# A hybrid decoder layer: a third tile for raw weights in the paired projections, two scratch rows claimed at once by each GLA pair, head 0's value parts issued behind the last sums of x, and two requeued steps in the DeltaNet part

## The chip, the cores and the metric

The kernel runs on one core of a Trainium2 chip. The metric is device time in microseconds of one execution, the median of several runs. PE is the matrix engine, DVE the vector engine, ACT the scalar engine, POOL the GpSimd engine and SP the engine that here only issues DMAs.

## The reference

One layer of a decoder: 512 tokens with 16 meta tokens ahead, width 2048. The normalised input goes through one combined projection, whose columns feed three kinds of heads; the gated results go through one output projection, a residual and a last norm.

```python
h = rms_norm(x, norm_w); h = pad(h)
proj = h @ w_in
(dq, dk, dv, dz, db, da, gq, gk, gv, gz, gl, fq, fk, fv, fz, ff) = split_cols(proj)
# A) 6 heads: gated DeltaNet (conv + SiLU on q, k, v; triangular solve in each chunk of 64)
o_dn = gated_head_norm(gated_delta_rule_chunked(q_dn, k_dn, v_dn, log_a, beta), dz, dn_norm_w)
# B) 5 heads: GLA, decay per key dimension
log_g = log_sigmoid(gl @ w_gk2 + b_gk) / 16
o_gla = gated_head_norm(gla_chunked(gq * 64**-0.5, gk, gv, log_g), gz, gla_norm_w)
# C) 5 heads: softmax attention with forget-gate bias, in blocks of 128 queries
o_fox = forgetting_attention(fq * 128**-0.5, fk, fv, log_f) * silu(fz)
return rms_norm(x + concat([o_dn, o_gla, o_fox]) @ w_out, final_norm_w)
```

All of it is float32. The chunk form of A needs the inverse of a lower triangular matrix per head and chunk.

## The kernel before

**Projections.** Each block of 128 projection columns is a product with K = 2048. A float32 operand is split into two parts, a rounded one and the rest (hi, lo), and three products of parts are summed: hi x hi, hi x lo of x, lo of the weights x hi. Weights come in halves of 128 x 1024: `load_half` (line 142) has SP load `raw`, ACT copy it into `whi` (line 162) and DVE subtract that into `wlo` (line 163). These two are put ahead of other work of their engines by a priority. The pool of these tiles, `wp`, holds two buffers of each name. `inproj` gives 96 matmuls for a block (line 220); a half-length matmul moves 264 columns, one without the meta tokens 512. `evac` brings the sum from PSUM to SBUF on DVE (line 338), `gate_z` does so for a gate (line 365) and applies SiLU through POOL and ACT (lines 347 to 351).

**Pairs of projections.** For heads 1 to 4 of the attention the blocks are computed two at a time by a scheme with seven products in place of eight (`inproj_pair`, line 505). `product` (line 513) is one of them: one `load_half`, then 24 matmuls (line 518). The scheme needs sums of halves of the weights, which POOL has added up in DRAM by DMA earlier (`ti`), and sums of halves of x: `x_sums` (line 472) prepares three sums per k and is called from the GLA pairs and head 0; `x_last` (line 493) then turns the second halves of x itself into differences, in place in `xh` and `xl`. Each k of `x_last` is a load on POOL (line 497), ACT 499, DVE 500, ACT 502, DVE 503. After it no ordinary projection may read that part of x, so it comes behind the last of them.

**The order of the work.** Two groups (g = 0, 1) of three DeltaNet heads come first. In each: gates, `dn_keys` (line 583), values, queries, `dn_inverse` (line 654), `dn_mix`. Then the gates of the GLA heads, three GLA pairs (`gla_pair`, line 860; the third pair has one head), and the attention heads (`fox_head`, line 1041). Independent chains run beside the projections on the other engines. Each engine works through a queue in order. A scheduler builds the queues from the written order and priorities; some matmuls are set behind a given projection matmul by hand (`behind`, `place`). A tile belongs to a buffer of its pool, and whoever first writes a new tile waits for the last users of the tile before it in that buffer. Of the tag `row` (128 x 531, scratch for one head's row) there are 7 buffers, of `six` (three rows) 14, of `t15` 6. PSUM has four banks for projections (`psb`) and four for all else (`psm`).

**DeltaNet keys.** `dn_keys` projects three key blocks with convolution and SiLU, then reads the decays `gb` from DRAM, broadcast over partitions (line 591, on ACT's queue), and forms the decay matrices on DVE from it: `atm` for the meta block and `at` for the four others (line 615), with ACT's exponentials (line 616).

**The inverse.** `dn_inverse` inverts the 32 x 32 diagonal blocks by elimination on DVE, writes them to DRAM and reads them back in two layouts, `xc` (a quarter of the tile `iv`) and `xm` (lines 682 and 684). DVE transposes both (lines 686, 687: `um`, `uc`), and matmuls `pm`, `pl`, `pn`, `pu` join the blocks.

**A GLA pair.** `gla_pair` projects keys and queries into the tile `gqk`, calls `x_sums`, projects two value blocks and turns them by PE (`pvg`, `pwg`, lines 853 and 856) into `gvt`. The gate's logarithms are computed in a row `u` with help of a row `t` (lines 883 to 892: `pgk` on PE, DVE, ACT, DVE). Then the scores come in seven steps (line 917 on): each has differences on DVE (922, 924), an exponential on ACT (925), products on DVE (926, 930) and small matmuls `pss` (944). The differences `d` stand in turn in the third part of `gvt` and in `u`. A third row, `spare`, is claimed ahead of the diagonal term (`psd`). After the scores: state updates (`pkd`, `pgm`, `pg`, `pgn`), the outputs `pgo` (lines 1008, 1014), the norm on ACT (1020 to 1025), and a transpose `pgt` (1028). SP reads the stored gate over the values in `gvt` (line 1031), DVE multiplies (1032) and SP stores the result in `zd` (1035).

**Attention head 0.** It uses ordinary projections: `fk`, `fv` into the row `vf`, `fq`, the gate `fz`, and head 1's `fk` and `fq` ahead. `values(v)` (line 1046) turns v by PE (`pvf`), splits it (`vhi`, `vlo`, `v3`, two rows and a small tile) and brings the meta values by `pwf`. The attention runs in four query blocks: logits `pfa` and `pfd` on PE (1118, 1119), the softmax on DVE and ACT (1122 to 1132), the transposes `pfx` (1135), the split of the probabilities (1138, 1139). After the blocks come `pfw` and the product `pfo`.

Of the kernel before, what the change touches and what calls it, by code (L numbers as in the profile page):

```python
# [8 lines left out]
F32 = mybir.dt.float32  # L9
# [9 lines left out]
P = 128  # L19
# [3 lines left out]
S = 512  # L23
T = NM + S
# [3 lines left out]
H = 3  # L28
# [54 lines left out]
def tile_hybrid_trunk(ctx, tc, xT, xtok, mtok, w_gate, w_in, w_out, w_dn, consts, lmask, fin_w, out, dbg=None):  # L83
# [57 lines left out]

    def load_half(src, name):
        raw = wp.tile([P, 1024], F32, tag="raw", name=f"raw{name}")
        nc.sync.dma_start(out=raw, in_=src)
        hi = wp.tile([P, 1024], F32R, tag="hi", name=f"whi{name}")
        lo = wp.tile([P, 1024], F32R, tag="lo", name=f"wlo{name}")
        split(raw, hi, lo)
        due[0] += rate[0]
        while due[0] > 0 and chores:
            cost = next(chores[0], None)  # L150
            if cost is None:
                chores.pop(0)
            else:
                due[0] -= cost
        return hi, lo
# [4 lines left out]
    def split(raw, hi, lo):  # L160
        with tc.high_priority(offset=1000000):
            pace[0] = A.copy(hi, raw).ins  # L162
            pace[1] = V.tensor_tensor(out=lo, in0=raw, in1=hi.bitcast(F32), op=ALU.subtract).ins  # L163

    pace = [None, None]

# [326 lines left out]
    def x_last():  # L493

        for k in range(NK):
# [7 lines left out]
            V.tensor_tensor(out=xl[k][:, HT:], in0=x22, in1=xh[k][:, HT:].bitcast(F32), op=ALU.subtract)  # L503

    def inproj_pair(n, c1, c2, tmp):

# [6 lines left out]
        def product(p_, src, xx, first=False, cols=slice(0, HT)):  # L513

            hi, lo = load_half(src, f"{b1}_{len(order)}")
            todo = [(hi, j, i) for j in range(NK) for i in range(2)] + [(lo, j, 0) for j in range(NK)]
            for i, (wt, j, part_) in enumerate(todo):
                m = PE.matmul(p_[:, cols], wt[:, j * P : (j + 1) * P], xx[j][part_][:, cols],  # L518
                              start=first and i == 0, stop=i == len(todo) - 1, skip_group_check=True)
                order.append(m.ins)  # L520
# [62 lines left out]
    def dn_keys(g):  # L583

        st = {}
        hs = range(H * g, H * g + H)
        kT = six.tile([P, H, T], F32, tag="six", name=f"kT{g}")
        for j, h in enumerate(hs):
            conv_silu(("dk", h), 6 + h, kT[:, j])
        gb = six.tile([P, H, T], F32, tag="six", name=f"gb{g}")  # L590
        nc.scalar.dma_start(out=gb, in_=gd[6 + H * g : 6 + H * g + H, :].partition_broadcast(P))
        kd = six.tile([P, NN, P], F32, tag="six", name=f"kd{g}")
# [61 lines left out]
    def dn_inverse(g, st):  # L654
# [30 lines left out]
        um = t15(f"um{g}", (32, H, 32))  # L685
        V.transpose(um.rearrange("p h c -> p (h c)"), xm.rearrange("p h c -> p (h c)"))
        V.transpose(uc.rearrange("p n c -> p (n c)"), xc.rearrange("p n c -> p (n c)"))

# [172 lines left out]
    def gla_pair(p):  # L861
# [12 lines left out]
        vt = vt3[:, :2, :S]  # L874
        V.memset(vt3[:, 0, 0:1], 0.0)
        x_sums(XSUM.get(p, ()))
        vm = t15(f"gvm{p}", (NM, 2, P))
        for e in range(ne):
            tok_values(inproj(("gv", 2 * p + e)), f"g{2 * p + e}", (vt3, qk)[e][:, 2], vt[:, e], vm[:, e])

        u = row(f"gu{p}")[:, :T][:R]
        t = row(f"gt{p}")[:, :T][:R]
        for a in range(2):
# [19 lines left out]

        spare = row(f"gpr{p}")[:, :S]
        prod = spare[:R]
# [7 lines left out]
        def scores(s, li):  # L913
            npair = S // (2 * s)
            kx, qx = kts[li % 2][:R], qts[li % 2][:R]
            v4 = lambda t_: t_.rearrange("p (n h s) -> p n h s", h=2, s=s)
            gv, kv, qv = v4(gc[:, NM:]), v4(kT[:, NM:]), v4(qT[:, NM:])
            kxv, qxv = v4(kx), v4(qx)
            d = (vt3[:R, 2, :S], u[:, :S])[li % 2]
            dv = v4(d)  # L920
            ref = gv[:, :, 0, s - 1 : s].to_broadcast([R, npair, s])
            V.tensor_tensor(out=dv[:, :, 1, :], in0=gv[:, :, 1, :], in1=ref, op=ALU.subtract)
            if s > 1:
                V.tensor_tensor(out=dv[:, :, 0, :], in0=ref, in1=gv[:, :, 0, :], op=ALU.subtract)
                A.activation(d, d, AF.Exp, scale=SC)
                V.tensor_tensor(out=kxv[:, :, 0, :], in0=kv[:, :, 0, :], in1=dv[:, :, 0, :], op=ALU.mult)
            else:
                A.activation(dv[:, :, 1, :], dv[:, :, 1, :], AF.Exp, scale=SC)
                kx = kT[:, NM:]
            V.tensor_tensor(out=qxv[:, :, 1, :], in0=qv[:, :, 1, :], in1=dv[:, :, 1, :], op=ALU.mult)  # L930
            return kx, qx
# [108 lines left out]
    def fox_head(h):  # L1040
# [24 lines left out]
        if h < H1:  # L1065
# [3 lines left out]
            x_sums(XSUM.get(3, ()))  # L1069
            vhi, vlo, v3, vm = values(v)  # L1070
            evac(inproj(("fq", h), meta=False), qT, scale=float(P) ** -0.5)
# [23 lines left out]
        if h < H1:  # L1095
            gate_z("fz", h, z)
            evac(inproj(("fk", H1)), ahead_[H1][:, 0])
            evac(inproj(("fq", H1), meta=False), ahead_[H1][:, 2], scale=float(P) ** -0.5)
            x_last()
        else:  # L1100
            zs["fz", h] = z
# [59 lines left out]
    XSUM = {1: (0, 1, 2), 2: (3, 4, 5), 3: (6, 7)}  # L1161
    PM = (308, 319)

# [42 lines left out]
    for h in range(FOX_HEADS):  # L1206
        dump(f"ofx{h}", zs["fz", h])

    for mm, n in later:
        n = head[n[0]] + n[1] if isinstance(n, tuple) else n  # L1210
# [278 lines left out]
```

## Time and profile before

| what | time |
|---|---|
| runs | 1049.26, 1045.46, 1046.46 us; median 1046.46 us |
| the profiled execution | 1053.94 us; from its first to its last instruction (its span) 1052.2 us |
| mean granted clock of TensorE in it | 0.969 of full speed |
| PE busy | 1006.0 us (96% of the span) |
| DVE, ACT, POOL busy | 656.3, 479.5, 236.2 us |
| bytes by DMA | 185.52 MB |

Every view below is of that one execution. Times in it are in us from its start unless a view says ns. A row of waits gives an engine and line, what its idle time was put down to, the total, how often and the longest; "SPq" and "ACTq" are DMA issues. A row of the timeline gives start, duration, engine, line, operation and tiles, and in brackets how long the engine had been idle and for what. A granted clock of 0.50 means that matmuls ran at half the rate; a busy PE is then not PE at its peak.

### The profile page before, as it was taken

What the parts mean: (1) busy time and instruction counts of PE and PEld (TensorE: products, weight loads), DVE (VectorE), ACT (ScalarE), POOL (GpSimd) and SP (SyncE); (2) the same over time, 40 slices, a digit from 0 to 9 for tenths busy, and PEclk for the clock granted to TensorE, in tenths of its full rate; (3) what the DMA queues carried; (4) which work ended last, traced back from release to release, by engine and by line L of the source; (5) the groups of instructions that cost most, each with busy time, mean ns of one, the idle gap of its engine ahead of it and who ended that gap; (6) DMA issues with size and microseconds to landing.
All of it is one profiled execution on the core that took longest, in us unless ns stands there. A gap on an engine that the chain in (4) does not pass through costs nothing.

```text
span 1052.2 us, 19776 instructions
## 1 busy us (share of the span) xinstructions
PE 1006.0 (96%) x7782; PEld 916.0 (87%) x7782; DVE 656.3 (62%) x1412; ACT 479.5 (46%) x1045; POOL 236.2 (22%) x272
## 2 busy tenths in 40 slices
PE   8999999989999999999999989869999999899996
PEld 7898999889999888999999868749999998688885
DVE  5356777855666984334493938465666675777573
ACT  6752533424446333234354544545444452534353
POOL 1032432413313343102213220222121212100051
PEclk9999999999999999999999987869999999999999
DMA  9744657767467798364858742433545556557434
GB/s 344 271 144 154 214 195 246 175 157 162 114 139 171 157 225 254 111 209 135 227 132 222 166 148 71 153 110 117 168 149 174 178 191 204 209 176 240 161 121 160
DMA packets 68225, 185.52 MB, mean 176 GB/s; under 512 B 13693, under 2 KB 16941, under 8 KB 67428
## 3 DMA queue, kind: packets, MB, share of 16 engines
q1 hardware_dynamic: 41776, 121.59, 34.4%
q0 software_dynamic: 15296, 52.63, 21.2%
q10 hardware_dynamic: 11060, 10.03, 3.2%
q8 instruction: 61, 1.00, 0.4%
q14 instruction: 32, 0.26, 0.1%
HBM read 173.81 MB, written 56.43 MB: 219 GB/s over the span
## 4 chain that ended last, share of the span: by engine, by line
PE 71%; DMA 6%; DVE 5%; ACT 3%; issue 3%; POOL 1%; ACTq 0%; DVEq 0%; POOLq 0%; SPq 0%
PE pp L220 36%; PE pp_a L518 6%; PE pq L1266 4%; PE pt L1266 3%; PE pa L1266 3%; PE ps L1266 2%; DVE wlo L163 1%; PE pp_b L518 1%; DMA accs<-in_xtok 1%; ACT whi L162 1%; DMA sc<-ab 1%; PE pp_d L518 1%; PE pp_c L518 1%; PE pr L1266 1%; PE pss L944 1%
## 5 line engine op out<-in xcount | busy, mean ns | idle before, releaser
L220 PE MATMUL pp<-xh,whi 128*128 128x264 f32 (+2 forms) x1120 | 275.9, 309 | 2.9 <-DVE vf L338 2.1
L220 PE MATMUL pp<-xh,wlo 128*128 128x264 f32 (+2 forms) x1120 | 271.8, 307 | 5.9 <-DVE wlo L163 5.9
L220 PE MATMUL pp<-xl,whi 128*128 128x264 f32 (+2 forms) x1120 | 274.0, 307 | 0.0
L162 ACT CAST whi<-raw 128x1024 fp32r<-128x1024 f32 x131 | 137.2, 1047 | 200.3 <-PE pp L220 100.0
L163 DVE TENSOR_TENSOR wlo<-raw,whi 128x1024 fp32r<-128x1024 f32 x131 | 164.2, 1254 | 84.2 <-ACT whi L162 67.6
L220 PEld LDWEIGHTS pp<-xh,wlo 128*128 128x128 f32 x1120 | 184.2, 191 | 15.1 <-DVE wlo L163 6.7
L220 PEld LDWEIGHTS pp<-xh,whi 128*128 128x128 f32 x1120 | 184.8, 191 | 12.4 <-DVE vf L338 2.5
L220 PEld LDWEIGHTS pp<-xl,whi 128*128 128x128 f32 x1120 | 184.8, 191 | 8.9 <-issue 0.2
L347 POOL TENSOR_SCALAR stc<-cv 128x528 f32<-128x528 f32 (+1 forms) x18 | 30.2, 1678 | 136.7 <-DVE cv L554 108.1
L1290 POOL TENSOR_TENSOR accs<-accs,fw 128x512 f32<-128x512 f32 x12 | 17.6, 1511 | 114.2 <-ACT sqf L1287 114.2
L518 PE MATMUL pp_a<-xh,whi 128*128 128x264 f32 x112 | 32.8, 320 | 9.3 <-ACT whi L162 4.6
L554 DVE SCALAR_TENSOR_TENSOR cv<-pb,cpk,cv 128x528 f32<-128x528 f32 (+1 forms) x54 | 41.1, 761 | 0.8
L518 PEld LDWEIGHTS pp_a<-xh,whi 128*128 128x128 f32 x112 | 23.6, 211 | 11.6 <-ACT whi L162 5.5
L518 PE MATMUL pp_a<-xl,whi 128*128 128x264 f32 x112 | 32.6, 319 | 0.9 <-DVE xl L503 0.9
L796 POOL TENSOR_TENSOR eg<-eg,qT 128x384 f32<-128x384 f32 x8 | 8.9, 1108 | 103.5 <-DVE egl L795 103.5
L518 PE MATMUL pp_a<-t,whi 128*128 128x264 f32 (+1 forms) x224 | 30.7, 289 | 0.1
L518 PEld LDWEIGHTS pp_a<-t,whi 128*128 128x128 f32 x224 | 29.2, 198 | 0.6 <-ACT fqk L539 0.5
L1266 PE MATMUL pa<-wloo,oh 128*128 128x512 f32 x72 | 29.4, 409 | 0.1
L1266 PE MATMUL pa<-whio,oh 128*128 128x512 f32 x72 | 27.0, 406 | 2.4 <-ACT whio L162 2.4
L1266 PE MATMUL pa<-whio,ol 128*128 128x512 f32 x72 | 28.9, 404 | 0.0
L162 ACT CAST whis<-raws 128x1024 fp32r<-128x1024 f32 x16 | 16.4, 1049 | 22.5 <-PE pq L1266 8.5
L347 POOL TENSOR_SCALAR stdz<-zdz 128x512 f32<-128x512 f32 x6 | 11.2, 1872 | 65.8 <-DVE zdz L365 65.2
(480 smaller groups left out, 2134.6 us busy)
## 6 DMA issues: line engine op xcount, KB each, us to landing
raw<-in_w_in SPq DMA_DIRECT2D x103, 512.0 KB, 3.7
ti<-in_w_in POOLq DMA_DIRECT2D x42, 512.0 KB, 5.6
raw<-ti SPq DMA_DIRECT2D x28, 512.0 KB, 3.3
tw<-in_w_dn POOLq DMA_DIRECT2D x24, 512.0 KB, 6.8
ti<-ti POOLq DMA_DIRECT2D x14, 512.0 KB, 6.5
rawo<-in_w_out SPq DMA_DIRECT2D x13, 512.0 KB, 3.8
raws<-tw SPq DMA_DIRECT2D x12, 512.0 KB, 4.2
xt<-in_xtok SPq DMA_DIRECT2D x8, 512.0 KB, 8.8
```

Of the source, the lines that this page charges most:

```text
L162: pace[0] = A.copy(hi, raw).ins
L163: pace[1] = V.tensor_tensor(out=lo, in0=raw, in1=hi.bitcast(F32), op=ALU.subtract).ins
L220: mm = PE.matmul(p_[:, :nt], wt[:, j * m : (j + 1) * m], xx[k][:, t0 : t0 + nt], start=(k == 0 and wt is hi and xx is xh), stop=(k == KT - ...
L347: G.tensor_scalar_max(t, src, LOW)
L518: m = PE.matmul(p_[:, cols], wt[:, j * P : (j + 1) * P], xx[j][part_][:, cols], start=first and i == 0, stop=i == len(todo) - 1, skip_grou ...
L554: V.scalar_tensor_tensor(out=c, in0=pb[:, t0 + w : w + T], scalar=cwc[:, blk, w : w + 1], in1=c, op0=ALU.mult, op1=ALU.add)
L796: G.tensor_tensor(out=eg, in0=eg, in1=qT[:, :, ts], op=ALU.mult)
L944: mm = PE.matmul(ps[o0 : o0 + n, b * n : b * n + n], kx[rr, k0 : k0 + n], qx[rr, q0 : q0 + n], start=True, stop=True)
L1266: PE.matmul(p_, o_[:, s], w_, start=(first and n == 0), stop=(last and n == 2), skip_group_check=True)
L1290: G.tensor_tensor(out=acc[tb, cc], in0=acc[tb, cc], in1=fw[cc], op=ALU.mult)
```

## The change

1. *A third tile for raw weights.* `load_half` takes an optional raw tile. `inproj_pair` counts its products, and every third one, for the pairs of heads 1 to 3, loads into one tile of the `six` pool, claimed in head 0 behind `x_sums`. Splits into hi and lo stay in two buffers each.
2. *GLA pairs.* The rows `trow` and `spare` are claimed together ahead of `x_sums`, each with a memset of one column on DVE that takes hold of the buffer. The row `u` is dropped: `u` is the third part of `gvt`. The differences of the score steps stand in turn in `u` and in `spare`.
3. *Head 0.* `values(v)` is called behind `x_last` in place of before the projection of `fq`.
4. *Decays.* For g = 0 the tile `gb` is claimed and loaded ahead of the key convolutions; for g = 1 it stays behind them.
5. *Inverse.* The transposes of `xm` and `xc` are set, on DVE, behind a split (line 163) counted from the place in the program where they are written: the 8th further on for g = 0, the 11th for g = 1.

No value that is computed changes.

```diff
+    raws = []
-    def load_half(src, name):
-        raw = wp.tile([P, 1024], F32, tag="raw", name=f"raw{name}")
+    def load_half(src, name, raw=None):
+        if raw is None:
+            raw = wp.tile([P, 1024], F32, tag="raw", name=f"raw{name}")
...
             pace[1] = V.tensor_tensor(out=lo, in0=raw, in1=hi.bitcast(F32), op=ALU.subtract).ins
+            splits.append(pace[1])
-    pace = [None, None]
+    pace, splits, waits = [None, None], [], []
...
+    third = [0]
...
-            hi, lo = load_half(src, f"{b1}_{len(order)}")
+            third[0] += 1
+            hi, lo = load_half(src, f"{b1}_{len(order)}", raws[0] if third[0] % 3 == 0 and h < FOX_HEADS - 1 else None)
...
+        def decays():
+            gb = six.tile([P, H, T], F32, tag="six", name=f"gb{g}")
+            nc.scalar.dma_start(out=gb, in_=gd[6 + H * g : 6 + H * g + H, :].partition_broadcast(P))
+            return gb
+        gb = decays() if g == 0 else None
         for j, h in enumerate(hs):
             conv_silu(("dk", h), 6 + h, kT[:, j])
-        gb = six.tile([P, H, T], F32, tag="six", name=f"gb{g}")
-        nc.scalar.dma_start(out=gb, in_=gd[6 + H * g : 6 + H * g + H, :].partition_broadcast(P))
+        gb = gb or decays()
...
-        V.transpose(um.rearrange("p h c -> p (h c)"), xm.rearrange("p h c -> p (h c)"))
-        V.transpose(uc.rearrange("p n c -> p (n c)"), xc.rearrange("p n c -> p (n c)"))
+        for o, x in ((um.rearrange("p h c -> p (h c)"), xm.rearrange("p h c -> p (h c)")),
+                     (uc.rearrange("p n c -> p (n c)"), xc.rearrange("p n c -> p (n c)"))):
+            waits.append((V.transpose(o, x).ins, len(splits) + SP[g]))
...
+        trow, spare = row(f"gt{p}"), row(f"gpr{p}")[:, :S]
+        for r in (trow, spare):
+            V.memset(r[:, 0:1], 0.0)
         x_sums(XSUM.get(p, ()))
...
-        u = row(f"gu{p}")[:, :T][:R]
-        t = row(f"gt{p}")[:, :T][:R]
+        u, t = vt3[:R, 2], trow[:R, :T]
...
-        spare = row(f"gpr{p}")[:, :S]
         prod = spare[:R]
...
-            d = (vt3[:R, 2, :S], u[:, :S])[li % 2]
+            d = (u[:, :S], spare[:R])[li % 2]
...
-            vhi, vlo, v3, vm = values(v)
+            raws.append(six.tile([P, 1024], F32, tag="six", name="raw3"))
+            V.memset(raws[0][:, 0:1], 0.0)
             evac(inproj(("fq", h), meta=False), qT, scale=float(P) ** -0.5)
...
             x_last()
+            vhi, vlo, v3, vm = values(v)
...
-    PM = (308, 319)
+    PM, SP = (308, 319), (8, 11)
...
+    for x, n in waits:
+        tc.add_manual_dep(x, splits[n].name, mybir.DependencyInfo(
+            mybir.DependencyClass.NoSync, mybir.DependencyReason.DATA), reason="behind")
```

## The prediction

> **What bounds the kernel now.** I read the page's head first, then the span in windows, then the waits of each stretch that the diff touches. In the page, PE is busy nearly always:
>
> ```profile
> span 1052.2 us, 19776 instructions
> PE 1006.0 (96%) x7782; PEld 916.0 (87%) x7782; DVE 656.3 (62%) x1412; ACT 479.5 (46%) x1045; POOL 236.2 (22%) x272
> ```
>
> So PE sets the end, and a saving counts only if it closes a gap of PE or gives back clock. The windows say where those are (columns: length; busy time of PE, PEld, DVE, ACT, POOL with counts; granted clock; DMA share; GB/s):
>
> ```profile
> 620.00:640.00 20.00, 15.56 (x81) 13.49 (x80) 12.24 (x29) 12.16 (x43) 1.50 (x1) 0.65 0.33 88
> 640.00:660.00 20.00, 20.00 (x241) 17.17 (x240) 15.74 (x37) 8.07 (x15) 0.59 (x1) 0.93 0.32 96
> 660.00:680.00 20.00, 16.20 (x149) 14.49 (x148) 8.42 (x12) 10.35 (x30) 3.15 (x4) 0.93 0.51 170
> 680.00:700.00 20.00, 13.40 (x55) 11.04 (x54) 11.92 (x38) 11.70 (x27) 6.96 (x10) 0.65 0.44 135
> 700.00:720.00 20.00, 16.09 (x83) 14.50 (x84) 9.60 (x30) 7.76 (x18) 3.17 (x3) 0.66 0.15 45
> ```
>
> From 620 to 720 (GLA pair 1's end, pair 2, head 0) PE idles 18.8 of 100 us and the clock averages 0.76. That is where most of the diff acts. The half-rate spells in it, by windows laid on their edges, and an earlier one:
>
> ```profile
> 626.00:643.00 17.00, 14.91 (x65) 13.85 (x66) 15.08 (x36) 7.60 (x18) 2.09 (x2) 0.50 0.13 44
> 677.00:697.50 20.50, 13.57 (x53) 11.43 (x54) 12.70 (x38) 10.80 (x27) 7.96 (x10) 0.58 0.51 163
> 701.00:714.60 13.60, 10.50 (x41) 9.05 (x40) 5.68 (x23) 3.83 (x8) 1.95 (x2) 0.50 0.18 60
> 229.90:233.30 3.40, 2.96 (x13) 2.96 (x14) 1.59 (x5) 3.32 (x6) 0.00 (x0) 0.50 0.54 167
> ```
>
> What a spell costs is PE's busy time in it times the missing clock: 14.91 x 0.50 = 7.5, 13.57 x 0.42 = 5.7, 10.50 x 0.50 = 5.3 and 2.96 x 0.50 = 1.5 us.
>
> The waits in 620 to 716 (waiter, what it waited for: total, times, longest):
>
> ```profile
> PE pfx L1135 <- DVE fmt L1130: 5.0, 2, 2.5
> PE pgt L1028 <- ACT gqk L1025: 4.1, 3, 1.9
> PE pp_a L518 <- ACT xh L502: 4.0, 2, 2.9
> PE pp_c L518 <- DVE zfz L365: 2.1, 1, 2.1
> PE pp L220 <- DVE vf L338: 2.1, 1, 2.1
> PE pp_a L518 <- DVE xl L503: 0.9, 1, 0.9
> PE pp_a L518 <- DVE vf L529: 0.6, 1, 0.6
> DVE gqk L1032 <- DMA gvt<-zd: 8.3, 1, 8.3
> ```
>
> **The change part by part.** Where I say how instructions stand in a queue after the change, it is from the built program's order.
>
> *GLA pairs.* With two rows claimed at the pair's start and u in the pair's own tile, pair 1's and pair 2's work moves about one projection block ahead. Between pgo and pgt, which wait for each other through ACT, PE now has only 7 projection matmuls in pair 1; after, 31. In pair 2 it is 48 for 9. At the pace of the row below (2.19 us for 16) 24 more matmuls are 3.3 us, more than the longest wait for ACT gqk, 1.9: the 4.1 goes. The two reads of gvt stand directly behind the pgo that free their buffer, so the DVE wait of 8.3 and PE's wait for vf behind it go: 2.1. zfz is evacuated ahead of pair 2's score chain on DVE: 2.1 for pp_c goes.
>
> ```profile
> 824.70 2.19 PE L518 MATMUL pp_d<-t,whi 128*128 128x264 f32 x16
> ```
>
> Cost of the claims: two memsets a pair and one for the raw tile, all on DVE in order. Those of pairs 0 and 1 move up to the second inverse and wait there for zd stores; the raw tile's waits for pair 1's two stores, with pair 2's gate chain queued behind it. The pairs' stores (line 1035, five of them) land in 2.0 to 4.1 us:
>
> ```profile
> DMA to landing us min/median/max: 2.0/3.4/4.1
> ```
>
> Some 4 us of DVE work stand between the last gqk and that memset, so I take 0 and keep 0 to 1.5.
>
> *x_last and head 0.* Now x_last's eight loads come on POOL behind stfz, and the first product that needs it waits 4.0 + 0.9:
>
> ```profile
> L497 POOL DMA_DIRECT2D xe<-in_xT x8: 722/723/823, 680.5 to 689.6; - x8
> L503 DVE TENSOR_TENSOR xl<-xe,xh x8: 424/426/434, 686.8 to 695.7; 128x264 fp32r<-128x264 f32 x8
> ```
>
> From the first issue to the last xl it takes 680.5 to 696.1, 15.6 us. After the change it is interleaved with pair 2's scores, with five products of 24 matmuls ahead of its use, some 16 us. But DVE then has both chains at once: from 640 to 720 it is busy 15.74 + 8.42 + 11.92 + 9.60 = 45.7 us, while PE's work in these 80 us is, at full clock, 20.00 x 0.93 + 16.20 x 0.93 + 13.40 x 0.65 + 16.09 x 0.66 = 53.0. DVE would have to be busy 86% of the time not to hold PE. I leave the 4.9 as it is (bounds: all of it gone; 10.7 more if x_last lies open).
>
> Head 0's values stand behind x_last, and its attention blocks 0 to 2 stand back to back on PE. Before, 11 matmuls lay between the pfa of block 1 and its pfx; block 2 had none, and shows what a bare block costs:
>
> ```profile
> 701.18 1.11 PE L1118 MATMUL pfa<-fqk 128*128 128x272 f32 x2
> 705.23 0.88 PE L1135 MATMUL pfx<-ident,fp 128*128 128x128 f32 x3 [2.50 <-DVE fmt L1130]
> ```
>
> Three bare blocks at 2.5 are 7.5, and DVE comes to the first with two weight splits (1.25 each, rows below) before it, of which I count 1.5: 9.0 in place of 5.0 + 0.6, so +3.4 (2 to 6).
>
> *Clock in this stretch.* The first spell begins behind the waits at 622 to 628, which go: -7.5. The second stands among pp_c's wait and those for x_last, of which one goes: half, -2.9. The third stands behind the pfx waits, which stay: 0. Sum of the stretch: -4.1 - 2.1 - 2.1 + 3.4 - 7.5 - 2.9 = -15.3 us (from +3 to -32).
>
> [...]
>
> *Third raw buffer.* Every third product of the pairs up to head 3 reads its weights from an own tile, so SP need not wait for the split two products back. With two buffers a load and a split must fit in two products, 2 x 24 matmuls, 6.6 us by the row above; they take 3.3 + 1.05 + 1.25 = 5.6 and more where the load is late:
>
> ```profile
> raw<-ti SPq DMA_DIRECT2D x28, 512.0 KB, 3.3
> L162 ACT CAST whi<-raw 128x1024 fp32r<-128x1024 f32 x131 | 137.2, 1047 | 200.3 <-PE pp L220 100.0
> L163 DVE TENSOR_TENSOR wlo<-raw,whi 128x1024 fp32r<-128x1024 f32 x131 | 164.2, 1254 | 84.2 <-ACT whi L162 67.6
> PE pp_a L518 <- ACT whi L162: 4.6, 4, 2.0
> ACT whi L162 <- DMA raw<-ti: 20.8, 11, 3.0
> ```
>
> The last two are waits of 720 to 880. ACT waits 20.8 us for loads, but PE feels 4.6. Head 4 keeps two buffers, so not all of it goes: -3.0 (0 to -4.6).
>
> *The inverse (g = 0).* DVE's transposes stand ahead of a weight split, and wait for iv:
>
> ```profile
> PE pp L220 <- DVE wlo L163: 3.5, 1, 3.5
> 228.45 0.58 DVE L687 STREAM_TRANSPOSE iv<-iv 128x384 f32<-128x384 f32 x1 [8.94 <-DMA iv<-sc]
> 229.11 1.17 DVE L163 TENSOR_TENSOR wlo<-raw,whi 128x1024 fp32r<-128x1024 f32 x1
> L693 PE MATMUL pm<-iv,an x48: 191/191/212, 233.9 to 234.7; 32*32 32x32 f32 x48
> ```
>
> After, that split goes first: PE's 3.5 (waits of 214 to 236) and the spell at 229.90, 1.5, go. Next late is pm, which waits for the transposes: PE reaches it 5.0 us earlier than its 233.9, at 228.9, and they still end at about 229.1; with the semaphores after them I say 0.7. Sum -4.3 (-2 to -5). For g = 1 the edit is the same, but x-sum loads now stand on POOL behind a zd store, and ACT behind them: I take 0, between one stall of this size more and one less (+3.5 to -3.5).
>
> *Decays (g = 0).* gb's read moves ahead of the key convolutions, some 3.5 us up on ACT's queue and past three POOL loads:
>
> ```profile
> 89.39 0.36 ACTq L591 DMA_DIRECT2D gb<-gd  x1
> 98.82 0.50 DVE L615 TENSOR_SCALAR atm<-gb,gcol 16x16 f32<-16x16 f32 x3 [4.95 <-DMA gb<-gd]
> DMA to landing us min/median/max: 5.2/7.3/9.4
> 91.98 1.22 DVE L163 TENSOR_TENSOR wlo<-raw,whi 128x1024 fp32r<-128x1024 f32 x1
> 95.99 0.41 PE L220 MATMUL pp<-xh,wlo 128*128 128x264 f32 x2
> 100.00:120.00 20.00, 16.78 (x134) 15.88 (x133) 13.45 (x26) 11.65 (x29) 7.07 (x8) 1.00 0.55 185
> ```
>
> PE idles 3.2 us at 100 to 120, behind the decays. Today the split of 91.98 runs before the atm, 2.8 us ahead of the matmuls of 95.99 that read it; after, it stands behind the atm, which wait for gb, and most of the decays. Issued near 86, gb lands at 91.2 to 95.4 (the third row is gb's two reads). Between the landing and the end of that split lie, by the DVE groups of this stretch, some 5 us of decays, keys and the split: ready at 96.2 to 100.4, so 0.2 to 4.4 lost against 3.2 saved. I take 0 (-3.0 to +1.2).
>
> Sum: -15.3 - 3.0 - 4.3 = -22.6. The profiled execution is 1052.2 + 1.7 = 1053.9, 7.5 above the median of 1046.46. I suppose that half of this, 3.7, lies in the half-rate stretches which the change shortens, so the median gains 22.6 - 3.7 = 18.9: **1027.5 us**, with 1018 to 1037 as this case's own range.
>
> **The rivals.**
> - *Slower: x_last and pair 2 hold each other up on DVE.* Both are chains through ACT and in-order DVE. If x_last's 15.6 lies open, PE waits 10.7 more than its 4.9, and the six products from pp_a to pp_a (144 matmuls of 0.13) run at half rate: +18.7. 1027.5 + 29.4 = 1057. For: DVE's 86%. Against: only a load's 3.3 us separates steps, and two rows take turns. It decides once the two exceed 24 us.
> - *The bare attention blocks keep the clock down.* Second spell whole and the third longer by the 20 matmuls of the next product: +2.9 + 2.6, and 6 in place of 3.4, +2.6; with the raw tile's wait, 1.5: 1037, and up to 1046 with the upper bounds of the other terms.
> [...]
> - *x_last is hidden wholly*: -4.9, and both later spells gone, -8.1: 1014.5.
> - *The third buffer does nothing*: ACT's wait for raw moves to the split, DVE or to the load itself: 1030.5.
>
> **How the numbers follow.** Likeliest 0.40; slower 0.16; bare blocks 0.15; short spells 0.12; hidden 0.10; no use of the buffer 0.07. A measurement of this kernel tells about 0.5%, 5.2 us, from no change, so faster means below 1041.2: all of the cases but the slower one and half of the bare blocks, 0.77; same 0.09 (that half and a little of the slower one); slower 0.14. The range goes from 1009 (below hidden) to 1046 and leaves out the slower case and a little below.
>
> **What would show it.** Right: no wait of DVE gqk for gvt above 2 us; no clock below 0.9 around the end of pair 1; in the first inverse no split behind iv and no half-rate spell behind it; waits of whi for raw<-ti below 10. The pfx waits should be 7 or more, the largest left. Wrong: a clock below 0.8 through pair 2's scores, with PE waiting for xh, xl or a split there; or pp waits for wlo near 100 above 4.

## The result: 1.3% faster

| | before | after |
|---|---|---|
| median of the runs | 1045.96 us | 1032.01 us |
| span of the profiled execution | 1052.2 us | 1032.7 us |
| mean granted clock | 0.969 | 0.985 |
| PE busy | 1006.0 us | 990.1 us |
| DVE busy | 656.3 us | 658.9 us |

The ratio is 0.9868, with a 95% interval of 0.9838 to 0.9898. The profiled execution of before took 1053.94 us, 8.0 above this median, and was a slow one, so sizes read from it are set below beside profiles of other kernels that leave the same stretch as it was. The forecast was 1027.5 us with a range of 1009 to 1046. So the time came out inside the range, 4.5 us above the point. How the gain is made up is another matter, and most of what follows is about that.

First the stretches that the change touches, as windows of before (columns as in the prediction):

```profile
215.00:235.00 20.00, 16.47 (x164) 16.08 (x163) 9.14 (x19) 6.50 (x11) 2.89 (x4) 0.91 0.56 141
500.00:612.00 112.00, 111.19 (x1485) 102.75 (x1484) 73.34 (x167) 54.07 (x134) 25.13 (x31) 1.00 0.72 184
620.00:720.00 100.00, 81.25 (x603) 70.69 (x602) 57.93 (x144) 50.05 (x132) 15.37 (x18) 0.76 0.35 107
720.00:860.00 140.00, 135.36 (x1074) 132.66 (x1073) 88.59 (x199) 70.14 (x130) 24.84 (x20) 0.99 0.52 171
```

and of after:

```profile
215.00:235.00 20.00, 19.83 (x291) 19.39 (x290) 7.91 (x14) 8.99 (x15) 6.58 (x9) 1.00 0.56 145
500.00:612.00 112.00, 104.18 (x1437) 94.83 (x1436) 70.70 (x164) 52.05 (x129) 26.65 (x30) 1.00 0.65 158
620.00:720.00 100.00, 84.66 (x736) 78.14 (x735) 66.61 (x162) 50.57 (x115) 19.35 (x21) 0.88 0.43 136
720.00:860.00 140.00, 138.59 (x1067) 133.48 (x1066) 93.37 (x203) 73.07 (x136) 25.58 (x21) 1.00 0.51 167
```

The windows stand at fixed times and the changed kernel is ahead, so a pair of rows holds not quite the same work. The reader sees four things. PE's idle time has fallen from 3.5 to 0.2 us in the first inverse (215 to 235) and from 4.6 to 1.4 in the pairs of projections (720 to 860). Around 620 to 720 the clock is 0.88 in place of 0.76 and PE idles 15.3 in place of 18.8 us. But between 500 and 612, in GLA pairs 0 and 1, PE now idles 7.8 us where it idled 0.8. And the second inverse (400 to 425) is a little worse, 1.7 us idle for 0.9.

The waits of after, from 590 to 702, beside the list in the prediction:

```profile
PE pfx L1152 <- DVE fmt L1147: 8.1, 3, 3.0
PE pss L959 <- DVE kq L945: 5.6, 3, 2.6
PE pss L959 <- issue: 1.2, 1, 1.2
PE pp_b L525 <- DVE fqk L342: 1.0, 1, 1.0
PE pp_a L525 <- DVE vf L536: 0.7, 1, 0.7
```

The waits for pgt's gqk, for zfz, xh and xl and the 2.1 for vf are all gone from this list. The one for pfx has grown from 5.0 to 8.1, and one is new: `pss`, the score matmuls of a GLA pair, waits for `kq`, the score operands that DVE makes. Two spells at half rate are left in this stretch, by windows on their edges:

```profile
654.00:664.20 10.20, 7.45 (x63) 6.59 (x64) 6.65 (x16) 6.17 (x17) 2.74 (x3) 0.50 0.47 133
684.70:698.40 13.70, 8.13 (x29) 6.71 (x30) 7.17 (x33) 3.39 (x9) 1.32 (x1) 0.50 0.01 2
```

### The profile page after: what moved, and what is told of

It reads as the page before. It is cut to its first block, busy times and chain, and to the rows that moved or that the text cites. A ratio compares the mean times of both kernels' runs of the same rounds, so it can differ in the third digit from the quotient of the medians.

```text
span 1032.7 us, 19789 instructions
## 1 busy us (share of the span) xinstructions
PE 990.1 (96%) x7782; PEld 903.3 (87%) x7782; DVE 658.9 (64%) x1419; ACT 480.3 (47%) x1045; POOL 237.1 (23%) x272
## 4 chain that ended last, share of the span: by engine, by line
PE 76%; DMA 10%; DVE 5%; ACT 3%; issue 3%; POOL 1%; SPq 0%; ACTq 0%; DVEq 0%; POOLq 0%
PE pp L224 35%; PE pp_a L525 6%; PE pq L1286 4%; PE pp L278 4%; PE pt L1286 4%; PE pa L1286 3%; PE ps L1286 2%; PE pp_b L525 2%; PE pp_c L525 2%; PE pp_d L525 2%; DVE wlo L166 1%; DMA xe<-in_xT 1%; DMA raw<-in_w_in 1%; ACT whi L165 1%; DMA accs<-in_xtok 1%
## 5 line engine op out<-in xcount | busy, mean ns | idle before, releaser
L224 PE MATMUL pp<-xh,whi 128*128 128x264 f32 (+2 forms) x1120 | 271.0, 306 | 2.6 <-issue 2.4
L224 PE MATMUL pp<-xh,wlo 128*128 128x264 f32 (+2 forms) x1120 | 268.1, 305 | 2.0 <-DVE wlo L166 2.0
L224 PE MATMUL pp<-xl,whi 128*128 128x264 f32 (+2 forms) x1120 | 268.2, 305 | 0.6 <-issue 0.6
L224 PEld LDWEIGHTS pp<-xh,whi 128*128 128x128 f32 x1120 | 181.3, 188 | 11.9 <-issue 2.8
L224 PEld LDWEIGHTS pp<-xh,wlo 128*128 128x128 f32 x1120 | 180.7, 189 | 11.5 <-DVE wlo L166 2.8
L224 PEld LDWEIGHTS pp<-xl,whi 128*128 128x128 f32 x1120 | 180.8, 189 | 9.8 <-issue 1.4
L525 PE MATMUL pp_a<-xh,whi 128*128 128x264 f32 x112 | 29.7, 298 | 2.0 <-ACT whi L165 1.3
L525 PE MATMUL pp_a<-xl,whi 128*128 128x264 f32 x112 | 29.3, 294 | 0.0
```

The costliest lines, as they stand in the source:

```text
L224: mm = PE.matmul(p_[:, :nt], wt[:, j * m : (j + 1) * m], xx[k][:, t0 : t0 + nt], start=(k == 0 and wt is hi and xx is xh), stop=(k == KT - ...
```

## The experiments

Each was measured beside the kernel before on the same chip, so ratios are to be compared, not microseconds: the kernel before ran at 1041 to 1043 us in these. A ratio of 0.990 is about 10 us.

### The two requeued steps alone

```diff
-        gb = six.tile([P, H, T], F32, tag="six", name=f"gb{g}")
-        nc.scalar.dma_start(out=gb, in_=gd[6 + H * g : 6 + H * g + H, :].partition_broadcast(P))
+        gb = gb or decays()        # for g = 0 called ahead of the key convolutions
...
+            waits.append((V.transpose(o, x).ins, len(splits) + SP[g]))
```

> The kernel before with only the two requeued steps: the decays of g = 0 loaded ahead of the key convolutions, and the inverse's transposes set behind a split. Theory (each part is worth what its own stretch of the two profiles shows): the waits near 100 go (3.2 us), in the first inverse 3.5 us of PE's wait and a spell of 3.4 us at half rate go, 1 to 2 us come back in the second inverse; 5 to 7 us faster than before, about 1040. Rival (the time won is eaten by the next wait, since the chains later in the kernel set the end): within 2 us of before.

Measured: ratio 0.9946 (0.9919 to 0.9972), 1036.79 for 1042.47, 5.7 us. The first inverse in this kernel:

```profile
215.00:235.00 20.00, 19.43 (x288) 18.88 (x287) 9.28 (x18) 10.18 (x16) 5.62 (x9) 1.00 0.62 153
```

The theory holds in size. PE's idle time in the first inverse goes from 3.5 to 0.6 us and the clock there from 0.91 to 1.00. The loss in the second inverse, which I expected here too, does not come: PE is busy all of the 25 us from 400 to 425. The changed kernel, profiled a second time beside later runs, does not show it either (PE busy 25.00 of the same 25 us), so it belonged to one execution.

How much of it is the decays? Four of the kernels below leave them as before, and in their profiles PE idles 0.4, 0.4, 0.4 and 0.9 us at 100 to 120, not the 3.2 of the profile before. One of them is the third raw tile alone; its window:

```profile
100.00:120.00 20.00, 19.59 (x162) 19.24 (x161) 13.46 (x32) 12.15 (x40) 7.42 (x13) 1.00 0.63 212
```

With the same code DVE's first use of gb starts at 93.96 here and at 98.82 in the profile before. So most of the 3.2 us belonged to that one execution. In the changed kernel it starts at 88.34 and PE's gap is gone, but it was mostly a gap of 0.4. No run has the decays alone.

From 612 to 720 this kernel has the code of the kernel before, and so it gives a second view of that stretch. PE's waits there are much as in the prediction's list (4.8 us for pfx, 4.0 for pgt, 3.1 for xh, 2.1 each for zfz and vf). Its half-rate spells there:

```profile
615.50:625.70 10.20, 7.70 (x32) 6.38 (x32) 7.63 (x18) 4.76 (x14) 0.00 (x0) 0.50 0.15 54
666.70:673.50 6.80, 6.11 (x28) 6.11 (x29) 2.03 (x5) 3.60 (x7) 5.04 (x6) 0.50 0.47 157
676.90:687.20 10.30, 7.47 (x26) 6.06 (x26) 6.52 (x28) 5.68 (x15) 2.15 (x4) 0.50 0.34 113
690.60:700.80 10.20, 7.12 (x27) 6.20 (x28) 4.85 (x22) 2.97 (x7) 1.94 (x2) 0.50 0.17 59
```

By PE's work in them they cost 28.40 x 0.50 = 14.2 us, and the first of them 3.9. In the profile of before it was 18.5, and 7.5 for the first.

### The third raw tile alone

```diff
+            raws.append(six.tile([P, 1024], F32, tag="six", name="raw3"))
+            V.memset(raws[0][:, 0:1], 0.0)
...
+            third[0] += 1
+            hi, lo = load_half(src, f"{b1}_{len(order)}", raws[0] if third[0] % 3 == 0 and h < FOX_HEADS - 1 else None)
```

> The kernel before with only the third tile for raw weights. Theory: PE's 4.6 us of waits for whi between 720 and 880 go except at most 1.5, and with them the spell at 837: 3 to 5 us faster, about 1042. Rival (the split, not the load, holds PE; what removed the waits in the changed kernel is the other order of head 0): within 1 us of before, and PE's waits for whi there stay above 3 us.

Measured: ratio 0.9965 (0.9932 to 0.9997), 3.6 us. The waits of this kernel between 720 and 880:

```profile
PE pp_a L524 <- ACT whi L165: 1.1, 2, 1.0
ACT whi L165 <- DMA raw<-ti: 9.6, 5, 3.1
```

PE's 4.6 us for whi became 1.1, ACT's 20.8 for raw became 9.6. The theory holds and the rival falls: it was the load. But the 4.6 was high: in the four other kernels here with two raw buffers PE waits 2.7 to 3.3 us, and ACT 15.9 to 19.4. The spell at 837 is gone too, but three of those four have none there either. The interval of the ratio leaves 0.3 to 7 us.

### The pairs and the values without the rest

The GLA part of the diff and the move of `values(v)`, and nothing else.

> The kernel before with only the rows of the GLA pairs claimed at once and head 0's values behind x_last. Theory: the stretch from the end of pair 1 to head 0 gains about 15 us, pairs 0 and 1 lose about 9 us to scores that come while DVE is busy, so 4 to 7 us faster, about 1041, with new waits of pss for kq. Rival (the parts depend on each other: without the third tile SP's loads come late beside the earlier scores): as slow as before or slower, 1046 to 1052.

Measured: ratio 0.9892 (0.9835 to 0.995), 1033.31 for 1042.47, 9 to 11 us, more than the 4 to 7 of the theory. Nothing was slower without the third tile; the rival falls. PE idles 6.4 us between 500 and 612, but no pss wait for kq, which the theory expected, is among its waits of 612 to 720. But the parts do not add up: 0.54%, 0.35% and 1.08% are 2.0% in sum, and the whole is 1.3%. The theory had a wrong idea of at least one of the two parts in this kernel, so the next runs take them apart.

### The changed kernel with the values put back

```diff
+            vhi, vlo, v3, vm = values(v)      # before the projection of fq, as it was
             evac(inproj(("fq", h), meta=False), qT, scale=float(P) ** -0.5)
...
             x_last()
-            vhi, vlo, v3, vm = values(v)
```

> The changed kernel with head 0's values put back before the projection of fq. Theory (the bare attention blocks cost PE about 3 us more than blocks with matmuls between them, but three of them stand bare in this build too, and the values' two rows are then held through x_last): pfx waits of 6 to 8 us remain, and x_last comes later: 0 to 5 us slower than the changed kernel, 1032 to 1037. Rival (the move of the values is what leaves the blocks bare): pfx waits of at most 5, 3 us faster, 1029.

Measured: ratio 0.9943 (0.9918 to 0.9968), 1037.41: some 7 us slower than the changed kernel (0.9868 and, below, 0.9875), more than the theory allowed, and not faster as the rival had it. Its waits from 612 to 720, the first two:

```profile
PE pfx L1152 <- DVE fmt L1147: 5.7, 2, 3.2
PE pp_a L525 <- ACT xh L506: 5.3, 3, 3.6
```

The pfx waits are smaller, between the 6 to 8 of the theory and the 5 of the rival, and x_last is late again, as in the kernel before.

### The changed kernel again, and with the pairs as before

> The changed kernel once more, on the chip of the three runs beside it. Theory (the parts' gains overlap: the pairs and the values already gave 1% alone): a ratio to before of 0.985 to 0.990. Rival (the parts add up, 0.5 + 0.35 + 1.1%, and the first measurement was low): 0.980 to 0.983.

Measured: ratio 0.9875 (0.9814 to 0.9937). The gains overlap; this interval alone reaches the rival's 0.983, the first one (0.9838 to 0.9898) does not.

```diff
-        trow, spare = row(f"gt{p}"), row(f"gpr{p}")[:, :S]
-        for r in (trow, spare):
-            V.memset(r[:, 0:1], 0.0)
...
-        u, t = vt3[:R, 2], trow[:R, :T]
+        u = row(f"gu{p}")[:, :T][:R]
+        t = row(f"gt{p}")[:, :T][:R]
...
+        spare = row(f"gpr{p}")[:, :S]
...
-            d = (u[:, :S], spare[:R])[li % 2]
+            d = (vt3[:R, 2, :S], u[:, :S])[li % 2]
```

> The changed kernel with the GLA pairs' rows claimed as before (u, t and spare where they were). Theory (the early claims give 8 us at the end of pair 1 and in pair 2 and cost 9 us between 500 and 600, so nearly nothing in all; the move of the values is what gains): within 4 us of the changed kernel, the waits of pgt and vf back at 620 to 628, PE's idle time between 500 and 600 below 3 us. Rival (the early claims are the gain): 8 to 14 us slower than the changed kernel.

Measured: ratio 0.9855 (0.9793 to 0.9917), 1028.33 against 1031.04 for the changed kernel beside it. Taking the GLA part out costs nothing that four runs of each can show (1024 to 1030 us without it, 1026 to 1032 with it); the rival, 8 us or more, falls. A window of the kernel with the pairs as before, and its waits from 612 to 720:

```profile
500.00:612.00 112.00, 111.14 (x1495) 102.00 (x1495) 73.41 (x169) 53.94 (x131) 25.55 (x30) 1.00 0.67 179
```

```profile
PE pfx L1151 <- DVE fmt L1146: 8.1, 3, 3.0
PE pgt L1042 <- ACT gqk L1039: 2.4, 2, 1.9
PE pp L224 <- DVE vf L342: 2.1, 1, 2.1
```

The waits of pgt and vf are back as expected, with a spell at 622 (last section), and PE idles 0.9 us between 500 and 612, where it was 7.8 in the changed kernel. And the waits for xh and xl, 4.9 us before, are not there although the pairs are as before. So it is the values that took them away.

### Pair 0's rows claimed late

```diff
-        trow, spare = row(f"gt{p}"), row(f"gpr{p}")[:, :S]
-        for r in (trow, spare):
-            V.memset(r[:, 0:1], 0.0)
+        if p:
+            trow, spare = row(f"gt{p}"), row(f"gpr{p}")[:, :S]
+            for r in (trow, spare):
+                V.memset(r[:, 0:1], 0.0)
         x_sums(XSUM.get(p, ()))
...
+        if not p:
+            trow, spare = row(f"gt{p}"), row(f"gpr{p}")[:, :S]
```

> The changed kernel with the rows of pair 0 alone claimed where they were before; pairs 1 and 2 as changed. Theory (the waits at 530 and 557 come from pair 0's scores moved ahead into time in which DVE is busy): 3 to 4 us less idle PE between 520 and 560, and 2 to 4 us faster than the changed kernel. Rival (they come from pair 1's earlier projections, which head 0's evacuation and the stores then hold): no difference there, within 1 us.

Measured: ratio 0.9917 (0.9882 to 0.9951): about 4 us slower than the changed kernel beside it (0.9875), with intervals that overlap. A miss. Its window of pairs 0 and 1, and its pss waits from 612 to 720:

```profile
500.00:612.00 112.00, 109.44 (x1453) 99.94 (x1452) 77.56 (x179) 55.38 (x135) 28.63 (x33) 0.98 0.67 175
PE pss L962 <- DVE kq L948: 9.9, 4, 5.8
```

PE idles 2.6 us between 500 and 612, where it was 7.8 in the changed kernel; 1.3 of that lies between 520 and 560, not the 3 to 4 expected. The wait of pss in pair 2 was 5.6 in the changed kernel and is 9.9 here, so most of what pair 0 no longer loses is lost there. PE's order in this profile shows how: from pair 2's first group of score matmuls at 641.87 to its last at 655.49 no projection matmul stands between the groups. Why the built program has this order, the run does not tell.

### x_last's subtractions on POOL

```diff
-            V.tensor_tensor(out=xl[k][:, HT:], in0=x22, in1=xh[k][:, HT:].bitcast(F32), op=ALU.subtract)
+            G.tensor_tensor(out=xl[k][:, HT:], in0=x22, in1=xh[k][:, HT:].bitcast(F32), op=ALU.subtract)
```

> The changed kernel with x_last's eight subtractions for xl on POOL in place of DVE: 8 x 0.42, 3.4 us off DVE in pair 2's scores. Theory (DVE's queue, with x_last between the score steps, is what PE's 5.6 us of pss waits for kq come from): these waits fall to 3 us or less, and with them the spell at 654 shortens; 2 to 6 us faster. Rival (the round trips through ACT and the loads set the pace, not DVE's work): pss waits of 5 us or more, within 1 us, or slower by up to 4 since each xl now waits in POOL's queue behind the loads of xe.

Measured: ratio 0.9888 (0.9819 to 0.9958), no difference to the changed kernel. Its pss wait:

```profile
PE pss L959 <- DVE kq L945: 5.5, 3, 2.4
```

The rival's sign came: with 3.4 us of work off DVE the waits are as before. That does not show that x_last's loads set the pace, though. In the changed kernel x_last has these waits (its engines for the loads, a load for the xl of two steps before, DVE for ACT's part of a step):

```profile
  DMA xe<-in_xT: 10.8, 5
  DVE xl L507: 8.1, 3
  ACT xe L503: 5.6, 5
```

In this run DVE waits 3.6 us for ACT's part in place of 5.6, and pss still waits 5.5. The run is not a clean test either, since one subtraction takes 0.76 us on POOL and 0.42 on DVE. PE's order in two traces tells more. Pair 2's last three groups of score matmuls in the changed kernel:

```profile
651.83 0.45 PE L959 MATMUL pss<-kq 64*32 64x32 f32 x32 [2.52 <-DVE kq L945]
652.71 0.45 PE L959 MATMUL pss<-kq,kq 64*32 64x32 f32 x32 [0.42 <-DVE kq L945]
655.80 0.65 PE L959 MATMUL pss<-kq,gqk 64*32 64x32 f32 x32 [2.64 <-DVE kq L945]
```

and the first and last of the three in the kernel with the pairs and the values and nothing else, with the longest row between them:

```profile
649.91 0.46 PE L945 MATMUL pss<-kq 64*32 64x32 f32 x32
650.83 2.10 PE L518 MATMUL pp_a<-t,whi 128*128 128x264 f32 x16
653.84 0.46 PE L945 MATMUL pss<-kq,gqk 64*32 64x32 f32 x32
```

There, too, pair 2's scores share DVE with x_last (waits of 10.7, 7.5 and 4.9 us in place of the 10.8, 8.1 and 5.6), and DVE is no faster: from the kq of the first of the three groups to that of the last it takes 4.9 us there (647.92 to 652.81) and 4.0 here (651.28 to 655.25). But there 25 projection matmuls stand between the last two groups and 35 ahead of the three, and PE does not wait; here it is none and 15. So PE waits because it is bare in front of a score step, as it is for pfx, and neither DVE's busy share, with which I reckoned in the prediction, nor x_last beside the scores is enough for it. Why the built program leaves these groups bare once the third tile and the requeued steps are there too, no run tells.

### The values alone, and the pairs alone

```diff
             x_sums(XSUM.get(3, ()))
-            vhi, vlo, v3, vm = values(v)
...
             x_last()
+            vhi, vlo, v3, vm = values(v)
```

> The kernel before with only head 0's values moved behind x_last. Theory (the values' two rows, free until then, give x_last more rows to load into, so its loads start right behind each other and earlier, and pp_a 3480 no longer waits for xh and xl; the kernel with the pairs as before is the fastest so far for this reason): the 4.9 us of these waits go, pfx waits rise from 5.0 to about 8, in all 3 to 7 us faster than before, a ratio of 0.993 to 0.997. Rival (the values gain only together with the early pairs): within 0.3% of before, or slower.

Measured: ratio 0.9908 (0.9885 to 0.993), 9.6 us, the largest part of all and above what I expected. The order of three steps in the kernel before (DVE, DVE, POOL, and x_last's first loads):

```profile
677.62 0.68 DVE L1054 TENSOR_TENSOR vlo<-pvf,vhi 128x512 fp32r<-128x512 f32 x1
678.22 0.68 DVE L365 TENSOR_TENSOR zfz<-pp,rstd 128x512 f32<-128x512 f32 x1
679.00 1.49 POOL L347 TENSOR_SCALAR stfz<-zfz 128x512 f32<-128x512 f32 x1 [11.54 <-DVE zfz L365]
680.45 2.28 POOL L497 DMA_DIRECT2D xe<-in_xT  x3
```

and with the values alone moved, with its pfx waits from 612 to 720:

```profile
640.71 0.68 DVE L365 TENSOR_TENSOR zfz<-pp,rstd 128x512 f32<-128x512 f32 x1
641.56 3.41 POOL L347 TENSOR_SCALAR stfz<-zfz 128x512 f32<-128x512 f32 x1 [7.69 <-ACT whi L162]
644.93 1.51 POOL L497 DMA_DIRECT2D xe<-in_xT  x2
```

```profile
PE pfx L1135 <- DVE fmt L1130: 8.5, 3, 3.3
```

In the kernel before, head 0's gate zfz stands on DVE right behind the values' vlo, and these wait for PE's pvf among pair 2's last transposes; the gate's work on POOL and x_last's loads stand behind zfz. With the values moved, zfz goes among pair 2's scores, and the loads begin at 644.93. In the kernel before it is 680.45, and 668.9 in the kernel with the two requeued steps alone, which has the same code here. So x_last starts 24 to 36 us earlier. pfx grew to 8.5, as expected; the waits for xh, xl and zfz are gone. That DVE's order was such because the seven rows were taken is my reading of the claims (vhi and vlo are two of the rows, zfz a third); no run here has an eighth row.

The pairs alone (the GLA part of the diff on the kernel before):

> The kernel before with only the GLA pairs' rows claimed at once (u, t and spare as in the changed kernel), head 0's values where they were. The prediction's step: the waits of pgt, vf and pp_c and the first half-rate spell go, 4.1 + 2.1 + 2.1 + 7.5 = 15.8 us, a ratio of 0.985. Theory now (those waits go, but 8 to 10 us come back in pairs 0 and 1, where the scores meet DVE at its busiest, and x_last stays where it was): within 4 us of before, 0.996 to 1.003.

Measured: ratio 0.9969 (0.9948 to 0.999), 3.2 us. Two of its waits from 612 to 720, its half-rate spells there and the window of pairs 0 and 1:

```profile
PE pgt L1029 <- ACT gqk L1026: 2.3, 1, 2.3
PE pp_c L518 <- DVE zfz L365: 2.1, 1, 2.1
```

```profile
661.10:671.30 10.20, 7.72 (x34) 7.32 (x35) 3.25 (x6) 5.04 (x12) 4.73 (x6) 0.50 0.35 119
674.70:685.00 10.30, 8.17 (x26) 6.18 (x26) 7.76 (x30) 6.00 (x16) 2.36 (x4) 0.50 0.35 115
688.40:698.60 10.20, 7.46 (x29) 6.53 (x30) 4.66 (x20) 3.31 (x7) 1.96 (x2) 0.50 0.12 35
```

```profile
500.00:612.00 112.00, 107.86 (x1470) 98.40 (x1468) 72.07 (x165) 54.21 (x146) 27.44 (x31) 1.00 0.67 165
```

The step as predicted (15.8 us) falls. Of the waits that I gave to it, the one for vf goes, pgt's falls from 4.1 to 2.3, and zfz's stays until the values move too. The first spell goes. But it costs 3.9 us and not 7.5 in the kernel with the requeued steps alone, and the three spells that are left cost 23.35 x 0.50 = 11.7 us, where the last three there cost 10.4; so the clock gives 2.5. And 3.3 us come back between 500 and 612 (4.1 idle for 0.8), not the 8 to 10 expected. x_last's loads begin at 667.0, as late as with the requeued steps alone (668.9).

### Matmuls between the attention blocks

```diff
             PE.matmul(pd[:, :P], qT[:, ts], kT[:, ts], start=True, stop=True)
+            if h == 0 and b in SPREAD:
+                ahead_of.append((mm.ins, len(order) + SPREAD[b]))
...
+    for x, n in ahead_of:
+        tc.add_manual_dep(order[n], x.name, mybir.DependencyInfo(
+            mybir.DependencyClass.NoSync, mybir.DependencyReason.DATA), reason="behind")
```

On the changed kernel, with `SPREAD = {0: 128, 1: 136}`:

> The changed kernel, with the last 16 matmuls of pp_a 3480 held back: 8 behind the logits of head 0's block 0 and 8 behind those of block 1, so that they stand between pfa and pfx. No matmul is added or left out. Theory (the 8.1 us of pfx waits are PE standing bare in front of DVE's and ACT's softmax chain, and the half-rate spell hangs on them): pfx waits at most 6.5, 2 to 4 us faster than the changed kernel (ratio to before about 0.985). Rival (the chain starts when DVE is done with the splits and the gate product, whatever PE holds back; the matmuls only move to another place): pfx waits of 7.5 or more, or the same time waited elsewhere; within 1 us of the changed kernel.

Measured: ratio 0.9883 (0.9857 to 0.991), as the changed kernel. pfx waits fell (first row); the window is the spell behind them:

```profile
PE pfx L1154 <- DVE fmt L1149: 5.6, 3, 2.5
```

```profile
682.60:696.30 13.70, 10.50 (x41) 9.04 (x40) 5.69 (x24) 3.83 (x8) 1.31 (x1) 0.50 0.12 40
```

By the waits the theory was right (8.1 to 5.6); by the time the rival was. The half-rate spell behind it is as long as before, 13.7 us, and has more of PE's work in it: 10.50 us in place of 8.13. The matmuls moved into the gaps, and ran there at half rate.

With the pairs as before and `SPREAD = {0: 96, 1: 112, 2: 128}`:

> The changed kernel with the GLA pairs' rows as before, and with 40 matmuls of products 3456 and 3480 held back between the logits and the transposes of head 0's blocks 0 to 2 (16, 8, 16). Theory (both edits take away waits that are PE's own): pfx waits below 5, the half-rate spell behind pair 2 shorter than 10 us, 1022 to 1026, a ratio to before of 0.978 to 0.984, faster than both kernels. Rival: the attention, moved ahead by a product, meets x_last and pair 2's gate product on DVE, and pp_a waits for xl or the splits instead: a ratio of 0.985 or more.

Measured: ratio 0.983 (0.9803 to 0.9857), 1024.57 us for 1041.19. It is the fastest of all, and its interval ends where that of the run beside it (0.9857 to 0.991) begins. Its second spell as a window, and its pfx waits:

```profile
680.90:687.70 6.80, 5.76 (x27) 5.51 (x27) 3.21 (x14) 2.26 (x4) 1.31 (x1) 0.50 0.09 35
```

```profile
PE pfx L1153 <- DVE fmt L1148: 4.9, 3, 2.2
```

With 40 matmuls over three blocks the spell is cut to 6.8 us; here both the waits and the clock give. How much of the time that is worth is not shown: with the pairs as before and nothing held back the ratio was 0.9855 (0.9793 to 0.9917), and the intervals overlap.

## Why the prediction was right, and where it was not

*The total* was forecast at -18.9 us against the median, and came at -13.9. *That PE sets the end, and that its gaps and its clock at 620 to 720 are the place,* holds.

*GLA pairs and the first spell* (-4.1 - 2.1 - 2.1 - 7.5 = -15.8). This is the step that failed. In the changed kernel the waits and the spell at 626 do go, as its profile shows. But alone the part is worth 3.2 us, and taken out of the whole it costs nothing measurable (0.9855 against 0.9875). Two things were wrong. The spell's 7.5 was read from one execution: in the kernel with the requeued steps alone the same spell costs 3.9, and with the pairs alone the clock gives only 2.5 in all. And I left out where the earlier work lands. PE idles 7.0 us more between 500 and 612; by its waits some 3.7 of the 7.8 there are for score matmuls and pgt, and for 3.0 the profile shows no cause. In pair 2, where score groups now stand bare on PE, 5.6 us of pss waits and a spell of 10.2 us arise. I had asked what hides the memsets, and not what hides the score chains themselves.

*The values* (+3.4). The size for the bare blocks was right: 9.0 us of pfx waits foretold, 8.1 found. But the same move also let the gate and x_last's loads go ahead, which I had left "as it is". So this step was charged as a loss of 3.4 and is a gain of 9.6 alone. By the parts alone the two errors are 12.6 and 13.0 us, in opposite directions. That they nearly cancel is why the total came out, and that was luck.

*x_last* (4.9 kept). The bounds held it, the value did not: the waits are gone, because the loads start earlier. "DVE would have to be busy 86%" argued from a busy share. Where PE does wait in pair 2, it is for pss, with nothing between the score groups, and 3.4 us of work taken off DVE left those waits as they were.

*Clock* (-7.5 - 2.9, and the third spell stays). The first spell is gone and the third stays, as forecast: 13.7 us, behind the pfx waits. The other one left stands in pair 2's scores. By work in them, 7.45 x 0.50 + 8.13 x 0.50 = 7.8 us are lost. Against the 18.5 of the profile of before that is 10.7 saved for 10.4 foretold, but against the 14.2 of the kernel with the requeued steps alone it is 6.4. The agreement belongs in part to one execution.

*Third raw tile* (-3.0): 3.6 alone. Its sign, waits of whi for raw<-ti below 10, came alone (9.6) and not in the changed kernel (11.8). *Inverse* (-4.3) *and decays* (0): 5.7 alone, of which the first inverse's gap and spell are 2.9 + 1.5; right within the interval. In the four other kernels that leave the inverse as it was, PE's wait for the split is 2.4 to 2.7 us, and only one of them has the spell. The 0 for the decays fits a gap of mostly 0.4; the 3.2 us of "saved" waits were of one execution. *Second inverse* (0): nothing that a second profile shows.

*The rivals.* "Short spells" (0.12) was an estimate of mine, that each spell left would be as short as the one at 229.90, 3.40 us; the two that are left in this stretch are 10.2 and 13.7 us. "Bare blocks" put the pfx waits 2.6 us above the 9.0 of the sum and made the third spell longer; they came to 8.1 us, and the spell of 13.7 is as long as before. "x_last hidden wholly" had its waits right: they went, but both later spells did not. The slower rival had its place right, pair 2's scores with x_last, but not what PE waits for: 5.6 us of pss and a spell that costs 3.7, in place of its 29.4. "The third buffer does nothing" falls with the 3.6. I moved half of 7.5 us between profile and median for the half-rate stretches; the 18.5 and 14.2 us of the two profiles differ by 4.3, which fits 3.7.

*What stays open.* The parts alone sum to 5.7 + 3.6 + 9.6 + 3.2 = 22.1 us, the whole is 13.8. The pairs and the values nearly add up, 12.8 alone and 11.2 together. Most is missing where these meet the third tile and the requeued steps: 11.2 + 3.6 + 5.7 = 20.5. One place of it shows in the traces, the bare score groups: PE idles 15.3 us between 612 and 720 in the changed kernel and 11.5 in the kernel with the pairs and the values alone. How the rest is spread can't be told within these intervals.

## What to carry to other kernels

Of a step that is moved away, ask who stood behind it in each queue and on its buffers, and not only what it costs at its new place: the largest gain here came from a gate and eight loads that no longer stood behind another step, in a move that looked like a loss on PE. When a chain is moved ahead, look at what stands between its steps on the engine that sets the end, and not only at how busy the other engines are there. Before a spell or a wait is priced from one profile, look for it in the profile of another kernel that has the same code there: here 7.5 us became 3.9. And before a change of several parts is explained, run each part alone: here one part of four, the one that changed most in the trace, gave nothing measurable beside the others.

## What the runs showed of the hardware

The half-rate spells whose rows stand above and in the prediction, all at a granted clock of 0.50 on their edges, lasted 3.4 us (before, at 229.90), 6.8 us (the two requeued steps alone, at 666.70; the pairs as before with matmuls held back, at 680.90), 10.2 to 10.3 us (eight, such as the changed kernel's at 654.00), 13.6 to 13.7 us (before, at 701.00; the changed kernel, at 684.70; matmuls between the attention blocks, at 682.60) and 17.0 us (before, at 626.00). What half rate is in matmuls shows in the kernel before: 128x264 projection matmuls start 0.22 us apart from 631.12 to 634.64, at a granted clock of 0.50, and 0.12 us apart from 221.81 to 226.40, at 1.00. In the kernel with the pairs as before, a spell of 10.2 us has PE busy all through:

```profile
622.00:632.20 10.20, 10.20 (x47) 9.71 (x46) 10.13 (x23) 5.11 (x11) 1.39 (x1) 0.50 0.15 52
```

What ends a spell is not shown by these runs; in this one the granted clock was 0.50 with PE busy 10.20 of 10.20 us.
